# Block-turned attention heads: the diagonal blocks copied by GpSimd, and one store for a tile's attention output

## The chip, the cores and the metric

The kernel runs on one core of a Trainium2 chip. The metric is device time in microseconds (us) of one execution; lower is better. The kernel before was timed three times: 2246.76, 2250.20 and 2251.48 us, median 2250.2 us.

## The reference

Two layers of a hybrid encoder are applied to a prompt of 1024 positions and a sample of 256 positions, all in float32. Each layer normalises its input, projects it once (`h @ w_in`), and runs four groups side by side: attention, a Fourier mix, spatial gating and a cross-attention into memory tokens. Each group is multiplied by a gate, the four are joined, projected by `w_out`, normalised and added to the input. The change touches the attention group alone:

```python
def self_attention(q, k, v):          # 8 query heads, 2 key/value heads, width 64
    ...
    def one_block(qblk):              # 128 queries at a time
        s = jnp.einsum('bqkgd,bskd->bkgqs', qblk, k, preferred_element_type=jnp.float32) * scale
        p = jax.nn.softmax(s, axis=-1)
        return jnp.einsum('bkgqs,bskd->bqkgd', p.astype(v.dtype), v)
    ...
o_att = self_attention(q, k, v) * jax.nn.silu(ag)
```

## The kernel before

The 1280 positions are ten tiles of 128: tiles 0 to 7 are the prompt, 8 and 9 the sample. Per layer the kernel does the spatial gating, the Fourier groups and the memory heads, then the projections for attention (`attention_qkv`, `attention_gates`), then the attention tiles (`attention`), and then the output product (`output`), which begins beside tiles 8 and 9. Results of the groups go to DRAM arrays `o_d[0..15]`, of 128 rows (channels) by 1280 positions each; `o_d[0..3]` are attention's. `output` reads them back (`load_o`, L910), attention's last.

In `attention` a prompt tile takes eight steps, one per head, in the order 2, 0, 3, 1, 6, 4, 7, 5 (L850). Heads 0 to 3 share key/value head `kv` 0, heads 4 to 7 `kv` 1; `j` is the head's number in its four. A step multiplies queries and keys on TensorE (`score`, L761), takes the row maximum on VectorE (L764) and the exponential on ScalarE (L766). Then the 128 by 1024 probabilities must be turned so that keys lie on the partitions (`turn`). Heads with `j` 0 or 1 are turned by TensorE (L791) and copied out by ScalarE (L796). Heads with `j` 2 or 3 are block-turned: VectorE's transpose (L776) turns only within 32 by 32 blocks and writes a tile `blocks`, and after the second of the two heads sixteen DMAs (L782) move `blocks` into `pd`, each 32 partitions by 2 KB (64 KB). Group `a` of 32 partitions and block `b` go to group `b` of `pd`; in the four moves of `r` = 0, `a` equals `b` and the partitions stay the same. So a prompt tile has 32 such DMAs, and a layer 256.

The product with the values (`values`, L833) of a tile runs during the steps of the tile after it, in four parts at steps 0, 2, 4 and 6 (L878 to 884). Parts 0 and 1 read `pt` (heads turned on TensorE), parts 2 and 3 read `pd`. The last part is followed by `finish`: VectorE multiplies the sum by the gate (L838), and four DMAs (L840) store the four 128 by 128 pieces into `o_d[0..3]`, 64 KB each.

All DMAs are issued by SyncE (SP) from one queue in order, so an issue that waits holds all behind it. That queue holds also the load of the next queries (L721, step 3) and of the gate (L800, step 4). GpSimd does two things per tile here: the low part of the queries (L727, step 1) and the spreading of the reciprocal row sums (L807, step 7).

`blocks` has two buffers (tag `a8`), `pt` and `pd` four together (`a16`). TensorE's order in this stage is the program's (L1056); the other engines' orders, SP's too, come out of a planner that simulates the program when it is built, so an operation that is moved can change the order of its neighbours.

Of the kernel before, what the change touches and what calls it, by code (L numbers as in the profile page):

```python
# [15 lines left out]
P = 128  # L16
# [3 lines left out]
SEQ = 1024  # L20
DEC = 256
# [53 lines left out]
def trunk_kernel(  # L75
# [10 lines left out]
    nc = tc.nc  # L86
# [11 lines left out]
    def a8(shape, dt=F32R):  # L98
        return sb.tile(shape, dt, tag="a8", bufs=2, name=uid("a8_"))

    def c4(shape, dt=F32):
        return sb.tile(shape, dt, tag="c4", bufs=N_C4, name=uid("c4_"))

    def c2(shape, dt=F32):
        return sb.tile(shape, dt, tag="c2", bufs=N_C2, name=uid("c2_"))
# [7 lines left out]
    def st(shape, tag="st", bufs=16):  # L113
        return sb.tile(shape, F32, tag=tag, bufs=bufs, name=uid("st_"))

    def mm(shape, dt=F32):
        return ps.tile(shape, dt, tag="mm", bufs=4, name=uid("mm_"))
# [18 lines left out]
    def dram(name, shape):  # L136
        return tc.dram_tile(shape, F32, name=name)

    def bcast(src, n):
        return src.unsqueeze(0).to_broadcast([P, n])  # L140
# [139 lines left out]
    def memory_prep(l, delay):  # L280
        gb = c4([P, D])
        nc.sync.dma_start(gb, bcast(mem_g[l], D))
        mT = [[c4([P, 2, 512], F32R) for _ in range(4)] for _ in range(2)]
        done = set()

        def put(mt, xs):
            pt = transpose_rows(xs)
            s = slice(mt * P, (mt + 1) * P)
            for k in range(4):
                split(mT[0][k][:, :, s], mT[1][k][:, :, s], pt[:, 2 * k:2 * k + 2, :])  # L290
            done.add(mt)
            S.tick(8 * TT)

        for mt in range(4):
            src = mem_prompt if mt < 2 else mem_sample
            x_sb = c4([P, D])
            nc.sync.dma_start(x_sb, src[(mt % 2) * P:(mt % 2 + 1) * P, :])
            xs = norm_rows(x_sb, gb)
            S.later(delay * (mt + 1), lambda mt=mt, xs=xs: put(mt, xs))
        return mT, done  # L300
# [81 lines left out]
    def fourier_setup(l):  # L382
        cs = c2([P, 2, P])
        nc.sync.dma_start(cs, c_dft)
        wf = c2([P, 4, P])
        nc.sync.dma_start(wf, w_fourier[l])
        pos = []
        for i in range(2):
            raw = wr([P, 2, 2, 256])
            nc.sync.dma_start(raw, c_pos[:, 2 * i:2 * i + 2])  # L390
            m = [c4([P, 2, 2, 256], F32R) for _ in range(2)]
            split(m[0], m[1], raw)
            pos += [[x[:, k] for x in m] for k in range(2)]
        cw = [c4([P, 4, 2, P], F32R) for _ in range(2)]
        for q in range(2):
            acc = s2([P, 4, P])
            nc.tensor.matmul(acc.rearrange("p g d -> p (g d)"), cs[:, q, :],
                             wf.rearrange("p g d -> p (g d)"), start=True, stop=True)
            split(cw[0][:, :, q, :], cw[1][:, :, q, :], acc)
        return cw, pos  # L400
# [139 lines left out]
    def memory_setup(l):  # L540
        out = []
        for src in (mk_d[l], mv_d[l]):
            hl = []
            for c in range(2):
                raw = wr([P, 2, 512])
                nc.sync.dma_start(raw, src[:, 2 * c:2 * c + 2])
                t = [c4([P, 2, 512], F32R) for _ in range(2)]
                split(t[0], t[1], raw)
                hl.append(t)
            out.append(hl)  # L550
        return out

    def memory_head(l, hT, h, o_d, mk, mv):
        w = slab("in", l, SLAB_MEM[h])
        for g in range(3):
            memory_unit(w, hT, h, g, o_d, mk, mv)
# [152 lines left out]
                S.tick(ROWS_COST)  # L709
        return q_d, kT, v8, v2  # L710

    def attention(l, q_d, kT, v8, v2, ag, o_d):

# [53 lines left out]
        def turn(t, h):  # L769
            e = tiles[t]  # L770
            kv, j = h // 4, h % 4
            p = e.pop(h)
            if e["prompt"] and j >= 2:
                if j == 2:
                    e["blocks"] = a8([P, 4, 8, 2, 32], F32)
                nc.vector.transpose(e["blocks"][:, :, :, j - 2].rearrange("p b k q -> p k b q"),  # L776
                                    p.rearrange("p (k b q) -> p k b q", b=4, q=32))
                if j == 3:
                    for r in range(4):
                        for a in range(4):  # L780
                            b = (a + r) % 4
                            nc.sync.dma_start(  # L782
                                e["pd"][32 * b:32 * b + 32, a, kv].rearrange("p k j q -> p (k j q)"),
                                e["blocks"][32 * a:32 * a + 32, b].rearrange("p k j q -> p (k j q)"))
                return
            for half in range(2 if e["prompt"] else 1):
                kn = 4 if e["prompt"] else 2
                pt = mm([P, 4, P])
                for kk in range(kn):
                    c0 = (half * 4 + kk) * P  # L790
                    nc.tensor.transpose(pt[:, kk, :], p[:, c0:c0 + P], ident)  # L791
                if e["prompt"]:
                    dst = e["pt"][:, half * 4:half * 4 + kn, kv, j, :]
                else:
                    dst = e["pt"][kv][:, :, j, :]
                nc.scalar.copy(dst, pt[:, :kn])  # L796
# [38 lines left out]
        def finish(t):  # L835
            e = tiles.pop(t)
            o = c2([P, 4, P])
            nc.vector.tensor_tensor(o, e["acc"], e["gt"], ALU.mult)  # L838
            for j in range(4):
                nc.sync.dma_start(o_d[j][:, t * P:(t + 1) * P], o[:, j, :])  # L840

        load_q(0)
        load_q(1)
# [11 lines left out]
        for n, (t, i, h) in enumerate(work):  # L855
# [14 lines left out]
            if i in (3, 5) and t + 1 < NT:  # L870
                turn_q(qhl, tiles[t + 1]["qT"], (i - 3) // 2)
            turn(t, h)
            if i == 7:
                for fs in todo:
# [142 lines left out]
        S.later(3.5 * (t - 1) - 9, lambda t=t: start_tile(t))  # L1017
    S.tick(0)
    for l in range(DEPTH):
        o_d = [dram(f"o{l}_{c}", [P, SEQ + DEC]) for c in range(16)]  # L1020
        cst = c4([P, 2, 4, P])
        nc.sync.dma_start(cst[:, 0], w_spatial[l])
        nc.sync.dma_start(cst[:, 1].rearrange("p h q -> p (h q)"), bcast(b_spatial[l], 512))
        vg = st([P, 4], tag="vg", bufs=1)
        nc.sync.dma_start(vg, v_g[l])
        sgu_pair(l, hT, 0, o_d, cst[:, 0], cst[:, 1], vg)
        four = []
        early = lambda: four.extend(fourier_setup(l))
        prep = []
        if l == 0:  # L1030
            sgu_pair(l, hT, 1, o_d, cst[:, 0], cst[:, 1], vg, lambda: prep.extend(memory_prep(0, 6)))
            m1 = memory_prep(1, 9)
            memory_kv(0, *prep, lambda: None)
            memory_kv(1, *m1, early)
        else:
            sgu_pair(l, hT, 1, o_d, cst[:, 0], cst[:, 1], vg, early)
        cw, pos = four
        for h in range(4):
            fourier_group(l, hT, h, o_d, cw, pos)
        mk, mv = memory_setup(l)  # L1040
        for h in range(4):
            memory_head(l, hT, h, o_d, mk, mv)
        q_d, kT, v8, v2 = attention_qkv(l, hT)
        ag = [dram(f"ag{l}_{t}", [P, 4, P]) for t in range(NT)]
        att = attention(l, q_d, kT, v8, v2, ag, o_d)
        gates = attention_gates(l, hT, ag)
        for i in range(7):
            next(gates)
            if i == 4:
                S.drain()  # L1050
        next(att)
        next(gates)
        last = l == DEPTH - 1
        out_hT = []
        out = output(l, o_d, xin if l == 0 else xmid, xout if last else xmid, out_hT)
        with tc.manual_schedule(engines={mybir.EngineType.PE}):  # L1056
            next(att)
            next(gates, None)
            for t, h in att:
                if t == 0 and h % 2 == 0:  # L1060
                    next(gates, None)
                if t >= 8:
                    next(out)
        for _ in out:
            pass
        hT = out_hT[0] if out_hT else None
# [89 lines left out]
```

## Time and profile before

| | us |
|---|---|
| median of three runs | 2250.2 |
| the profiled execution, its own time | 2251.54 |
| its span in the trace | 2249.5 |
| TensorE busy (matmul) | 2161.9 (96%) |
| VectorE busy | 1124.4 (50%) |
| ScalarE busy | 852.9 (38%) |
| GpSimd busy | 243.6 (11%) |
| mean granted TensorE clock | 0.987 |

Times in the trace count from the start of the span. An instruction is named by engine, line and the tiles that it writes and reads. A number in square brackets behind an instruction is the time for which its engine stood idle before it, with what ended the wait. "PE" is TensorE, "PEld" its weight loads, "DVE" VectorE, "ACT" ScalarE, "POOL" GpSimd, "SPq" the queue of SyncE. The prompt's attention tiles lie at about 715 to 938 us in layer 0 and 1776 to 2003 us in layer 1.

### The profile page before, as it was taken

Reading aid. Unit: us, or ns where it says so; the run is one execution under the profiler, and the core shown is the slowest. Engines: PE = TensorE matmul, PEld = TensorE weight load, DVE = VectorE, ACT = ScalarE, POOL = GpSimd, SP = SyncE. Lnnn points to the kernel's source line nnn. Section 1 sums busy time; section 2 is a strip of 40 time slices with the busy share of each in tenths; the row PEclk is TensorE's granted clock in tenths of the full one; section 3 lists DMA queues with packets and bytes.
Section 4 is the critical chain, followed back from the end, with each engine's and each line's share of the span. In section 5 each row is a group of like instructions: output and inputs, shape, how many; then the busy total and the mean of one; then the engine's idle time right before and its main releaser. Section 6 shows DMA issues by size and latency. Waiting matters only on the chain.

```text
span 2249.5 us, 33414 instructions
## 1 busy us (share of the span) xinstructions
PE 2161.9 (96%) x12872; PEld 1842.0 (82%) x12872; DVE 1124.4 (50%) x1972; ACT 852.9 (38%) x1935; POOL 243.6 (11%) x416
## 2 busy tenths in 40 slices
PE   7999999999999988999999999999999988999997
PEld 7898988888998656678888988888899866667885
DVE  6344344445573666534464343445467365643445
ACT  6133332334322656542264222234342365654121
POOL 2010000000141000000062000000014000000005
PEclk9999999999999999999999999999999998999999
DMA  4123321201122544532342121021112344453234
GB/s 172 59 97 131 131 92 57 99 31 55 59 78 69 129 115 122 146 103 85 103 163 86 57 80 57 31 99 42 51 55 79 91 111 110 123 146 99 91 106 140
DMA packets 120782, 210.95 MB, mean 94 GB/s; under 512 B 20400, under 2 KB 55600, under 8 KB 120624
## 3 DMA queue, kind: packets, MB, share of 16 engines
q1 hardware_dynamic: 120624, 208.82, 29.9%
q8 instruction: 102, 1.67, 0.3%
q14 instruction: 56, 0.46, 0.1%
HBM read 129.05 MB, written 46.14 MB: 78 GB/s over the span
## 4 chain that ended last, share of the span: by engine, by line
PE 76%; SPq 9%; DMA 5%; DVE 4%; issue 2%; ACT 2%; POOL 2%; DVEq 0%; POOLq 0%; ACTq 0%
PE mm L248 34%; PE mm L926 13%; PE mm L261 12%; SPq L782 7%; PE mm L833 3%; PE s L761 3%; PE mm L311 2%; PE mm L327 1%; PE s L422 1%; PE s L408 1%; PE s L576 1%; DMA wr<-o 1%; PE mm L609 1%; DMA a<-a 1%; SPq L840 1%
## 5 line engine op out<-in xcount | busy, mean ns | idle before, releaser
L248 PE MATMUL mm<-a,ws 128*128 128x512 f32 (+1 forms) x4032 | 795.1, 355 | 0.0
L248 PEld LDWEIGHTS mm<-a,ws 128*128 128x128 f32 x4032 | 663.6, 189 | 102.5 <-issue 0.5
L926 PE MATMUL mm<-ws,a 128*128 128x512 f32 x1632 | 380.6, 392 | 2.6 <-ACT c L933 2.6
L926 PEld LDWEIGHTS mm<-ws,a 128*128 128x128 f32 x1632 | 303.9, 188 | 67.4 <-ACT c L933 3.6
L261 PE MATMUL mm<-ws,a 128*128 128x256 f32 x2400 | 302.0, 286 | 0.0
L261 PEld LDWEIGHTS mm<-ws,a 128*128 128x128 f32 x2400 | 294.8, 194 | 0.5 <-DVE a L234 0.2
L764 DVE TENSOR_REDUCE st<-s 128x1 f32<-128x1024 f32 (+1 forms) x160 | 170.0, 1063 | 148.8 <-PE s L761 148.7
L833 PE MATMUL mm<-a,c 128*64 128x256 f32 x1024 | 148.0, 413 | 41.3 <-DMA a<-a 41.2
L273 ACT ACTIVATE c<-mm 128x512 f32<-128x512 f32 (+1 forms) x96 | 50.7, 528 | 322.8 <-PE mm L248 319.0
L766 ACT ACTIVATE c<-s,st 128x1024 f32<-128x1024 f32 (+1 forms) x160 | 159.0, 994 | 35.7 <-DVE st L764 34.9
L761 PE MATMUL s<-c,c 128*128 128x512 f32 (+1 forms) x576 | 167.8, 410 | 2.5 <-ACT c L766 1.9
L274 DVE SCALAR_TENSOR_TENSOR c<-c,mm 128x512 f32<-128x512 f32 (+1 forms) x96 | 57.2, 595 | 217.8 <-ACT c L273 217.8
L833 PEld LDWEIGHTS mm<-a,c 128*64 128x64 f32 x1024 | 77.7, 145 | 100.8 <-issue 59.1
L166 ACT ACTIVATE ws<-wr,pre_g 128x256 fp32r<-128x256 f32 x304 | 126.6, 505 | 22.2 <-DMA wr<-in_w_in_dram 16.0
L761 PEld LDWEIGHTS s<-c,c 128*128 128x128 f32 x576 | 101.7, 194 | 37.7 <-issue 18.4
L167 DVE SCALAR_TENSOR_TENSOR ws<-wr,pre_g,ws 128x256 fp32r<-128x256 f32 x304 | 128.6, 483 | 2.6 <-ACT ws L166 2.5
L935 DVE TENSOR_TENSOR c<-c,mm 128x512 f32<-128x512 f32 x120 | 80.9, 682 | 83.9 <-PE mm L926 83.9
L148 POOL TENSOR_SCALAR st<-st 128x1 f32<-128x1 f32 (+3 forms) x120 | 26.7, 223 | 743.5 <-DVE st L654 453.4
L150 POOL TENSOR_TENSOR st<-st,mhalf 128x1 f32<-128x1 f32 (+3 forms) x120 | 99.8, 832 | 9.9
L776 DVE STREAM_TRANSPOSE a<-c 128x1024 f32<-128x1024 f32 x64 | 79.2, 1237 | 31.9 <-DMA a<-a 27.7
L144 DVE TENSOR_TENSOR ws<-wr,ws 128x1024 fp32r<-128x1024 f32 x48 | 57.0, 1221 | 67.0 <-ACT ws L143 66.9
L143 ACT CAST ws<-wr 128x1024 fp32r<-128x1024 f32 x48 | 48.1, 1049 | 101.6 <-PE mm L926 84.4
(120 smaller groups left out, 2213.7 us busy)
## 6 DMA issues: line engine op xcount, KB each, us to landing
wr<-in_w_in_dram SPq DMA_DIRECT2D x76, 512.0 KB, 4.3
a<-a SPq DMA_DIRECT2D x512, 64.0 KB, 2.0
wr<-in_w_out_dram SPq DMA_DIRECT2D x32, 512.0 KB, 4.4
wr<-o SPq DMA_DIRECT2D x64, 256.0 KB, 3.0
c<-in_x_prompt_dram SPq DMA_DIRECT2D x16, 512.0 KB, 6.2
o<-c SPq DMA_DIRECT2D x32, 256.0 KB, 2.0
wr<-in_w_mem_kv_dram SPq DMA_DIRECT2D x16, 512.0 KB, 4.1
q<-c SPq DMA_DIRECT2D x40, 128.0 KB, 1.7
```

Source lines behind the costliest of these rows:

```text
L150: nc.gpsimd.tensor_tensor(r, m, mhalf[:, :n], ALU.pow)
L166: nc.scalar.activation(w[:, 0, kk], raw[:, k], AF.Copy, scale=g)
L167: nc.vector.scalar_tensor_tensor(w[:, 1, kk], raw[:, k], g, fv(w)[:, 0, kk], ALU.mult, ALU.subtract)
L248: nc.tensor.matmul(acc[:, :n], w[:, a, k, c * P:(c + 1) * P], hT.t[g][b][:, k, :], start=i == 0, stop=i == 3 * KC - 1)
L261: nc.tensor.matmul(acc[:, :256], hT.t[g][a][:, k, tt * P:(tt + 1) * P], w[:, b, k, :], start=i == 0, stop=i == 3 * KC - 1)
L761: nc.tensor.matmul(s[:, c0:c0 + n], e["qT"][:, h, :], kT[kg][b][:, kv, :], start=b == 0, stop=b == 1)
L764: nc.vector.tensor_reduce(nm, s[:, :nk], axis=AX.X, op=ALU.max, negate=True)
L766: nc.scalar.activation(p[:, :nk], s[:, :nk], AF.Exp, bias=nm, accum_out=e["rs"][:, j, kv:kv + 1])
L782: nc.sync.dma_start(e["pd"][32 * b:32 * b + 32, a, kv].rearrange("p k j q -> p (k j q)"), e["blocks"][32 * a:32 * a + 32, b].rearrange("p ...
L833: nc.tensor.matmul(out, vt, src, start=kt == 0, stop=kt == last)
L926: nc.tensor.matmul(acc, oT[g][c][:, a, tt * P:(tt + 1) * P], w[:, b, c, :], start=j == 0, stop=j == 11)
L935: nc.vector.tensor_tensor(ys, ys, acc, ALU.add)
```

## The change

The four DMAs with `r` = 0 become four GpSimd copies, in the same loop and for the same data; the twelve others stay DMAs of SP. The array of attention's output becomes one DRAM array of 128 by 4 by 1280, and `finish` stores a tile by one DMA of 256 KB (128 partitions, four runs of 512 B each) in place of four. `output` reads the same pieces as before, from slices of that array.

```diff
-    def attention(l, q_d, kT, v8, v2, ag, o_d):
+    def attention(l, q_d, kT, v8, v2, ag, o_att):
...
                     for r in range(4):
                         for a in range(4):
                             b = (a + r) % 4
-                            nc.sync.dma_start(
-                                e["pd"][32 * b:32 * b + 32, a, kv].rearrange("p k j q -> p (k j q)"),
-                                e["blocks"][32 * a:32 * a + 32, b].rearrange("p k j q -> p (k j q)"))
+                            dst = e["pd"][32 * b:32 * b + 32, a, kv].rearrange("p k j q -> p (k j q)")
+                            src = e["blocks"][32 * a:32 * a + 32, b].rearrange("p k j q -> p (k j q)")
+                            if r == 0:
+                                nc.gpsimd.tensor_copy(dst, src)
+                            else:
+                                nc.sync.dma_start(dst, src)
...
-            for j in range(4):
-                nc.sync.dma_start(o_d[j][:, t * P:(t + 1) * P], o[:, j, :])
+            nc.sync.dma_start(o_att[:, :, t * P:(t + 1) * P], o)
...
-        o_d = [dram(f"o{l}_{c}", [P, SEQ + DEC]) for c in range(16)]
+        o_att = dram(f"o{l}_att", [P, 4, SEQ + DEC])
+        o_d = [o_att[:, c, :] for c in range(4)] + [dram(f"o{l}_{c}", [P, SEQ + DEC]) for c in range(4, 16)]
```

## Rows read from the trace of the kernel before

**Rows 1.** The page: busy time, and the chain that ended last by line.

```profile
PE 2161.9 (96%) x12872; PEld 1842.0 (82%) x12872; DVE 1124.4 (50%) x1972; ACT 852.9 (38%) x1935; POOL 243.6 (11%) x416
...
PE mm L248 34%; PE mm L926 13%; PE mm L261 12%; SPq L782 7%; PE mm L833 3%; PE s L761 3%; PE mm L311 2%; PE mm L327 1%; PE s L422 1%; PE s L408 1%; PE s L576 1%; DMA wr<-o 1%; PE mm L609 1%; DMA a<-a 1%; SPq L840 1%
```

**Rows 2.** The waits: engine, line, waited for, us in total, times, longest.

```profile
PE mm L833 <- DMA a<-a: 41.2, 14, 4.4
...
DVE a L776 <- DMA a<-a: 27.7, 13, 3.8
```

**Rows 3.** Busy time by stretch: from wait to wait, six tiles a layer, then two single ones.

```profile
core 0: us, PE busy (x) PEld busy (x) DVE busy (x) ACT busy (x) POOL busy (x), PEclk, DMA share, GB/s
...
764.41:914.63 150.22, 129.98 (x840) 89.49 (x841) 96.59 (x92) 93.06 (x168) 11.37 (x12) 0.97 0.47 116
1826.24:1979.37 153.13, 135.38 (x840) 92.75 (x841) 95.78 (x91) 90.07 (x165) 11.36 (x12) 0.92 0.46 114
...
764.41:789.12 24.71, 20.88 (x140) 14.48 (x141) 16.00 (x16) 15.76 (x29) 1.90 (x2) 1.00 0.49 118
...
1878.55:1905.69 27.14, 23.69 (x141) 16.06 (x141) 15.99 (x16) 15.01 (x27) 1.89 (x2) 0.88 0.44 108
```

**Rows 4.** Busy time by stretch, as rows 3, after the last wait of each layer.

```profile
914.63:938.20 23.57, 23.26 (x138) 16.44 (x139) 10.81 (x16) 10.70 (x26) 1.91 (x2) 0.93 0.49 121
1979.37:2003.00 23.63, 23.32 (x138) 16.56 (x139) 11.80 (x17) 12.84 (x30) 1.90 (x2) 0.93 0.47 116
```

**Rows 5.** Timeline of SP's queue over one tile of layer 0: start, us, instruction.

```profile
837.51 10.04 SPq L782 DMA_DIRECT2D a<-a  x15
847.66 0.53 SPq L721 DMA_DIRECT2D c<-q  x1
848.23 0.46 SPq L800 DMA_DIRECT2D c<-ag  x1
848.78 0.51 SPq L782 DMA_DIRECT2D a<-a  x1
849.39 1.98 SPq L840 DMA_DIRECT2D o<-c  x4
851.42 12.10 SPq L782 DMA_DIRECT2D a<-a  x18
```

**Rows 6.** All issues of L782: duration in ns (min/median/max), and time to landing.

```profile
L782 SPq DMA_DIRECT2D a<-a x512: 507/589/1923, 735.3 to 2002.5; - x171
...
DMA to landing us min/median/max: 1.9/2.0/4.7
```

**Rows 7.** Timeline of VectorE in the same tile: last of `kv` 1, `finish`, next `kv` 0.

```profile
844.94 1.24 DVE L776 STREAM_TRANSPOSE a<-c 128x1024 f32<-128x1024 f32 x1
...
847.94 0.68 DVE L838 TENSOR_TENSOR c<-mm,c 128x512 f32<-128x512 f32 x1
...
854.53 1.23 DVE L776 STREAM_TRANSPOSE a<-c 128x1024 f32<-128x1024 f32 x1
```

**Rows 8.** Timeline of TensorE at the wait of that tile, and at one in tiles 8, 9.

```profile
858.81 0.65 PE L833 MATMUL mm<-a,c 128*64 128x256 f32 x2
863.11 2.84 PE L833 MATMUL mm<-a,c 128*64 128x256 f32 x14 [3.65 <-DMA a<-a]
...
2015.94 3.01 PE L926 MATMUL mm<-ws,a 128*128 128x512 f32 x12 [1.60 <-ACT c L933]
```

**Rows 9.** Timeline of GpSimd and VectorE where they work at the same time, attention.

```profile
822.16 0.61 POOL L807 COPY c<-st 128x512 f32<-128x512 f32 x1 [17.06 <-DVE st L805]
822.27 1.22 DVE L764 TENSOR_REDUCE st<-s 128x1 f32<-128x1024 f32 x1 [0.17 <-PE s L761]
...
827.06 1.23 DVE L764 TENSOR_REDUCE st<-s 128x1 f32<-128x1024 f32 x1 [0.34 <-PE s L761]
827.33 1.28 POOL L727 TENSOR_TENSOR c<-c,c 128x512 fp32r<-128x512 f32 x1 [4.57 <-ACT c L726]
```

**Rows 10.** The same at the end of layer 0, and the durations of L959.

```profile
1152.15 1.29 POOL L951 TENSOR_TENSOR c<-c,c 128x512 f32<-128x512 f32 x1
1152.22 2.43 DVE L959 SCALAR_TENSOR_TENSOR c<-c,st,c 128x512 f32<-128x512 f32 x2 [1.22 <-POOL st L150]
...
L959 DVE SCALAR_TENSOR_TENSOR c<-c,st,c x40: 737/751/1783, 1130.9 to 2245.5; 128x512 f32<-128x512 f32 x40
```

More of the change, by code (lines that the diff above doesn't have):

```diff
@@ L1044, in trunk_kernel @@
         ag = [dram(f"ag{l}_{t}", [P, 4, P]) for t in range(NT)]
-        att = attention(l, q_d, kT, v8, v2, ag, o_d)
+        att = attention(l, q_d, kT, v8, v2, ag, o_att)
         gates = attention_gates(l, hT, ag)
```

## The prediction

> **What bounds the kernel now.** I read the page first. TensorE is busy for 96% of the span, so as a whole this is a TensorE kernel; but in the chain that ended last, one line of SP's queue, L782, has 7% of the span [rows 1]. 7% of 2249.5 us is 157 us in which the end of the program hung on SP issuing the block moves. That is a share of the chain and not a gain: if the issues go faster, TensorE's own work takes their place. So the second view is the waits: TensorE stood still for the block moves 14 times, 41.2 us in all, always at L833; VectorE waited 27.7 us for the same moves before its block transposes (L776), since `blocks` has two buffers [rows 2].
>
> The third view is the stretches from one wait's end to the next. Twelve of them, six a layer, hold a tile each. They last 303.35 us (150.22 + 153.13) of which TensorE is busy 265.36 (129.98 + 135.38); the difference, 38.0 us, is twelve of the fourteen waits, and 3.2 us are the first of each layer [rows 3]. The same 140 matmuls take 20.88 us at a granted clock of 1.00, which is 2.4 GHz, and up to 23.69 us where it was 0.88, so that a part of the stretch went at 1.2 GHz [rows 3]. TensorE did nothing else in those stretches than in the others; what came before the lower clock is the wait. VectorE has 16.0 us of work per tile and ScalarE 15.0 to 15.8, less than TensorE's 20.88, so neither would hold a tile of 20.9 us.
>
> The fourth view is SP's queue in one tile [rows 5]. It is full: 15 block moves from 837.51 to 847.55, the two loads, one move, the four stores, and 18 moves from 851.42. That is 0.67 us for a move (10.04 / 15, and 12.10 / 18), 1.98 us for the stores, 0.53 and 0.46 for the loads. 32 x 0.67 + 1.98 + 0.99 = 24.4 us per tile, and the stretch at full clock lasts 24.7 us [rows 3]. So **in the prompt's attention SP's issuing is the bound, and TensorE, which needs 20.9 us, waits for the rest.**
>
> **The change, part by part.**
>
> *Four of sixteen moves leave SP.* Per tile 24 moves stay: 24 x 0.67 = 16.1 us, with the loads and the store (below) 17.5 to 19.1 us. That is under 20.9, so SP has a reserve and TensorE becomes the bound. But a reserve on average isn't enough, the moves of `kv` 1 must land in time. I follow one tile through three views [rows 5, 7, 8]. Its `kv` 1 blocks are ready at 846.18 (L776 at 844.94 for 1.24). TensorE asks for them at 859.46, the end of the two matmuls at 858.81, so it can give them 13.3 us. Before, SP was still at work on `kv` 0 at 846.18, sent one move at 848.78 and the others from 851.42; TensorE went on at 863.11. After, the `kv` 0 moves (12 x 0.67 = 8.0 us) and the loads (1.0 us) fit in the 11.3 us between the `kv` 0 blocks (one period of 20.88 before 854.53 + 1.23, so 834.88) and 846.18; SP is free then. If the planner keeps its order, one move goes first, then the store, which must wait for L838 (till 847.94 + 0.68 = 848.62), and eleven moves are queued behind that wait. The store's issue takes 0.46 to 1.98 us (below), so the eleven begin at 849.1 to 850.6, the last 10 x 0.67 later, at 855.8 to 857.3, and it lands 2.0 us after its issue [rows 6]: 857.8 to 859.3. TensorE asks at 859.46. **The waits of 41.2 us go, with 0.2 to 1.7 us to spare.** What is late next is nothing that I can see for those 20.9 us: the stretch at full clock has no other wait. VectorE's wait of 27.7 us goes too; it counts for nothing of its own, since TensorE waited at the same time.
>
> *TensorE's clock.* The twelve stretches at full clock would be 12 x 20.88 = 250.56 us of TensorE's work in place of 265.36, so 14.8 us go as well if the clock stays at 1.00 [rows 3]. After the last wait of each layer comes another stretch at 0.93, 23.3 us busy [rows 4]; 7% of that is 1.6 us each, 3.2 us. Bounds: none of these 18.0 us comes back, or all. I take all, because the stretch from 764.41, behind one of the two first waits (1.6 us in the mean), ran at 1.00 [rows 3], and I expect no longer ones.
>
> *The copies on GpSimd.* A copy writes 512 elements per partition. The nearest row is L807, a copy of 512 per partition, 0.61 us; the upper end is L727 with two inputs, 1.28 us [rows 9]; the lower end is nothing, since only 32 partitions are busy. Four take 2.4 us (0 to 5.1) and are done 849 to 851, ahead of the twelve DMAs, which hide them. That cover is 13.3 us wide; it would be used up only at 3.3 us a copy. Per tile GpSimd gets 4.9 us on top of 1.9 [rows 3]. Behind the copies in its queue stand L807, which may come 2.4 us later (TensorE reads its result at step 2 of the next tile, two steps on), and L727, not needed for two steps either. Cost 0.
>
> *Four stores become one.* No store or load of the trace has four runs per partition. Lower end: the cost of L800, a load of 256 KB with one run per partition, 0.46 us [rows 5]; upper end: the four stores as before, 1.98 us. What SP saves here is at most 1.5 us per tile, and hidden once SP isn't the bound. I take the middle; both ends are in the walk above. When it lands doesn't matter: L910 reads it after the products of the three other groups.
>
> *What stays.* At tiles 8 and 9 TensorE waits for loads of the output product that stand behind the last moves in SP's queue (one of 1.60 us [rows 8]). SP gets there earlier by 2.7 us (4 x 0.67) and TensorE too. I keep back 3.0 us for waits that come up there.
>
> *A rule against it.* Where GpSimd and VectorE worked at once with L764, L764 took 1.22 and 1.23 us, as alone [rows 9]. Where VectorE had two inputs in SBUF, at the layer's end, two L959 beside L951 took 2.43 us in place of 2 x 0.75 [rows 10]. In attention no VectorE operation has two SBUF inputs. The Trainium skill, page "SBUF — State Buffer", section "SBUF: two separate sides", says that VectorE and GpSimd share a pair of ports by an exclusive lock, and that the loser blocks fully. By the rows the copies cost VectorE nothing, by that rule taken without its condition they would cost what the third rival has; the L959 rows agree with the rule.
>
> *Sum.* 41.2 + 14.8 + 3.2 - 3.0 = 56.2 us. The profiled execution had 2251.54 us, its span lacks 2.0 of it: 2251.5 - 56.2 = 2195.3. The median of the runs lies 1.3 us below the profiled one: **2194 us**.
>
> **The rivals.**
>
> 1. *A wait remains.* The planner puts the store ahead of all twelve moves and its issue is dear: 850.6 + 11 x 0.67 + 2.0 = 860.0, 0.5 us late; with one long issue (up to 1.92 us for 0.59 [rows 6]) 1.8. For it: the margin was 0.2 us at the dear end. Against: at the cheap end it is 1.7. Some 1.3 us at 14 places give 18 us back, with the clock at 1.00 as after the first waits: 2212 us; with half of the clock's loss 2221.
> 2. *Nothing changes.* The moves' landing and not their issue sets the time, so fewer issues help nothing: 2250 us. Against: landing takes 2.0 us while the issues stand back to back for 24.4, and the DMA engines are busy 0.47 [rows 3]. The skill's page "DMA: Bandwidth & Descriptors", section "Issuing engines are not separate DMA queues", calls the saving in issue time usually small beside the DMA itself; these rows speak against that here.
> 3. *Slower: the copies hold VectorE.* If they lock L764 and L776 out, 8 copies x 0.61 = 4.9 us per tile fall into VectorE's order, which sets off each exponential. It decides once more than 59.2 / 16 = 3.7 us of these count. All of it: 16 x 4.9 = 78 us, 2272 us. Against: rows 9. For: no row shows L776 beside GpSimd.
>
> **How the numbers follow.** Forecast 0.70, first rival 0.18, second 0.03, third 0.06; 0.03 for a planner's order that costs some us, still faster. The range holds the forecast with its ends: 2194 less the 3.0 kept back, less 3.2 if waits like the 1.60 us go in both layers, less 3.4 for the fastest run before (2246.8 against 2250.2), gives 2184; the first rival at its dear end, 2221, and 3 more give 2224. A measurement here tells 0.2% (4.5 us) from no change. Faster: 0.70 + 0.18 + 0.03 = 0.91, same 0.03, slower 0.06.
>
> **What would show it.** Right: no wait of L833 for block moves over 1.3 us, tiles of 20.9 to 21.5 us, granted clock 0.98 or more in both prompt stretches, gaps in SP's queue. The part on order is wrong if the waits stay at L833 with the store just ahead of the moves; the part on copies if L764 or L776 grow beyond 1.25 us, or L833 waits for GpSimd. A tile still at 24 us would make the whole reading wrong.

## The result and the profile after

The changed kernel takes 2190.87 us in the median of four runs (2188.82 to 2192.31), against 2250.84 us before. The ratio is 0.9741, with a 95% interval of 0.9724 to 0.9757. The profiled execution had 2190.76 us, 60.8 us less than the one before; the prediction's sum was 56.2. The predicted time was 2194 us.

TensorE's busy share rose to 98%. SP's line of the block moves, 7% of the chain that ended last in [rows 1], is no longer among the parts that the page lists; the chain is TensorE's. The page of the changed kernel, busy time and the chain by line:

```profile
PE 2140.2 (98%) x12872; PEld 1832.7 (84%) x12872; DVE 1122.5 (51%) x1972; ACT 853.1 (39%) x1935; POOL 324.7 (15%) x544
...
PE mm L248 35%; PE mm L928 16%; PE mm L261 12%; PE s L761 6%; PE mm L836 5%; PE mm L794 3%; PE mm L311 2%; PE mm L327 1%; PE s L422 1%; PE s L408 1%; PE s L576 1%; PE mm L609 1%; POOL c L953 1%; PE s L217 1%; DVE c L961 1%
```

The values product is line 836 now, the block moves that are left are line 787, the copies 785, the store 842, `finish`'s multiplication 841. In the groups of instructions of the changed kernel (busy time, mean ns | idle time before them, and what ended it) the values product waits 5.2 us in all, for ScalarE, where it waited 41.2 us for DMAs [rows 2]. VectorE's block transpose, which waited 27.7 us for DMAs, waits for none:

```profile
L836 PE MATMUL mm<-a,c 128*64 128x256 f32 x1024 | 127.9, 389 | 5.2 <-ACT a L799 5.2
...
L776 DVE STREAM_TRANSPOSE a<-c 128x1024 f32<-128x1024 f32 x64 | 79.0, 1235 | 2.5 <-ACT c L766 2.5
```

The stretches that answer to [rows 3 and 4], in the changed kernel: one tile, the passage from tile 7 to tile 8 in layer 0, six tiles of layer 1 less 0.8 us, and the passage in layer 1 (length, TensorE busy, ..., granted clock, DMA share, GB/s):

```profile
781.77:802.05 20.28, 20.28 (x142) 14.29 (x141) 15.72 (x16) 15.01 (x27) 6.76 (x11) 1.00 0.46 116
...
882.40:908.00 25.60, 22.27 (x131) 15.57 (x130) 16.08 (x24) 17.67 (x40) 8.15 (x10) 0.93 0.59 162
1794.60:1915.50 120.90, 120.90 (x839) 85.17 (x838) 93.77 (x90) 89.68 (x161) 40.28 (x60) 1.00 0.46 116
1915.50:1940.00 24.50, 20.74 (x125) 14.44 (x124) 15.55 (x23) 16.19 (x35) 7.13 (x9) 0.93 0.60 164
```

A tile takes 20.28 us, all of it TensorE's work, at 2.4 GHz throughout. At the passage to tile 8 TensorE is idle for 3.3 and 3.8 us of the stretch, and part of it runs at 1.2 GHz.

SP's queue over one tile of the changed kernel, beside [rows 5], then VectorE and GpSimd at the end of the `kv` 1 blocks, and TensorE's product that reads them:

```profile
781.33 11.13 SPq L787 DMA_DIRECT2D a<-a  x13
792.55 0.57 SPq L842 DMA_DIRECT2D o_att<-c  x1
793.18 6.97 SPq L787 DMA_DIRECT2D a<-a  x11
800.25 0.52 SPq L721 DMA_DIRECT2D c<-q  x1
800.87 0.40 SPq L803 DMA_DIRECT2D c<-ag  x1
...
790.68 1.23 DVE L776 STREAM_TRANSPOSE a<-c 128x1024 f32<-128x1024 f32 x1
791.84 0.65 DVE L841 TENSOR_TENSOR c<-mm,c 128x512 f32<-128x512 f32 x1
...
791.98 2.56 POOL L785 COPY a<-a 32x512 f32<-32x512 f32 x4 [8.04 <-DVE a L776]
794.60 0.61 POOL L810 COPY c<-st 128x512 f32<-128x512 f32 x1
797.45 1.28 POOL L727 TENSOR_TENSOR c<-c,c 128x512 fp32r<-128x512 f32 x1 [2.24 <-ACT c L726]
...
804.58 1.73 PE L836 MATMUL mm<-a,c 128*64 128x256 f32 x14
```

The blocks are ready at 791.91. One move is issued, the store follows at 792.55, and eleven moves take 6.97 us (0.634 each): the last starts at 799.5 and lands at about 801.5, with the 2.0 us of [rows 6]. TensorE's own chain reaches the product that needs it at about 804.9, the second pair of matmuls after 804.58. SP rests ahead of each set of blocks (13 moves at 0.634 are 8.2 of the 11.13 us in the first row); its issues come to 24 x 0.634 + 0.57 + 0.92 = 16.7 us of a tile's 20.28. The four copies are done at 794.5.

### The profile page after: what moved, and what is told of

Its sections match the earlier page's. It is cut to its first block, busy times and chain, and to the rows that moved or that the text cites. A ratio compares the mean times of both kernels' runs of the same rounds, so it can differ in the third digit from the quotient of the medians.

```text
span 2189.0 us, 33399 instructions
## 1 busy us (share of the span) xinstructions
PE 2140.2 (98%) x12872; PEld 1832.7 (84%) x12872; DVE 1122.5 (51%) x1972; ACT 853.1 (39%) x1935; POOL 324.7 (15%) x544
## 4 chain that ended last, share of the span: by engine, by line
PE 87%; DMA 3%; DVE 3%; ACT 3%; POOL 2%; issue 2%; SPq 1%; DVEq 0%; POOLq 0%; ACTq 0%
PE mm L248 35%; PE mm L928 16%; PE mm L261 12%; PE s L761 6%; PE mm L836 5%; PE mm L794 3%; PE mm L311 2%; PE mm L327 1%; PE s L422 1%; PE s L408 1%; PE s L576 1%; PE mm L609 1%; POOL c L953 1%; PE s L217 1%; DVE c L961 1%
## 5 line engine op out<-in xcount | busy, mean ns | idle before, releaser
L261 PE MATMUL mm<-ws,a 128*128 128x256 f32 x2400 | 304.2, 287 | 0.0
L261 PEld LDWEIGHTS mm<-ws,a 128*128 128x128 f32 x2400 | 296.8, 195 | 0.5 <-DVE a L234 0.2
L764 DVE TENSOR_REDUCE st<-s 128x1 f32<-128x1024 f32 (+1 forms) x160 | 170.0, 1062 | 123.2 <-PE s L761 123.2
L836 PE MATMUL mm<-a,c 128*64 128x256 f32 x1024 | 127.9, 389 | 5.2 <-ACT a L799 5.2
L836 PEld LDWEIGHTS mm<-a,c 128*64 128x64 f32 x1024 | 68.8, 137 | 55.7 <-issue 19.7
L785 POOL COPY a<-a 32x512 f32<-32x512 f32 x128 | 80.2, 627 | 199.1 <-DVE a L776 141.7
L953 POOL TENSOR_TENSOR c<-c,c 128x512 f32<-128x512 f32 x40 | 55.8, 1395 | 272.8 <-ACT c L948 272.7
```

Source lines behind the costliest of these rows:

```text
L261: nc.tensor.matmul(acc[:, :256], hT.t[g][a][:, k, tt * P:(tt + 1) * P], w[:, b, k, :], start=i == 0, stop=i == 3 * KC - 1)
L764: nc.vector.tensor_reduce(nm, s[:, :nk], axis=AX.X, op=ALU.max, negate=True)
L785: nc.gpsimd.tensor_copy(dst, src)
L836: nc.tensor.matmul(out, vt, src, start=kt == 0, stop=kt == last)
```

## The experiments

Each was timed beside the kernel before. The table gives the ratio with its 95% interval, and what the values product, and that line alone, waited for in the profile.

| run | us | ratio | values product waits, us |
|---|---|---|---|
| changed kernel | 2190.87 | 0.9741 [0.9724, 0.9757] | 5.2, ScalarE |
| copies alone | 2192.55 | 0.9739 [0.9716, 0.9761] | 1.9, ScalarE |
| store alone | 2235.93 | 0.9933 [0.9908, 0.9957] | 30.8, block moves |
| two copies of four | 2198.85 | 0.9774 [0.9751, 0.9797] | 2.8, block moves |
| four moves issued by GpSimd | 2190.50 | 0.9729 [0.9713, 0.9746] | 4.9, ScalarE |
| tiny DMAs added | 2201.28 | 0.9778 [0.9764, 0.9793] | 12.5, DMAs |
| copies three times | 2280.02 | 1.0131 [1.0111, 1.0150] | 55.4, GpSimd |
| dear copies | 2191.78 | 0.9739 [0.9724, 0.9753] | 2.6, ScalarE |
| later product | 2190.31 | 0.9732 [0.9717, 0.9746] | 5.1, ScalarE |
| splits on GpSimd | 2185.51 | 0.9712 [0.9696, 0.9727] | none |
| changed kernel again | 2187.39 | 0.9717 [0.9701, 0.9733] | the same two waits, 2.2 and 2.4 |

**Copies alone.** The copies stay, the store is four DMAs again.

```diff
-            nc.sync.dma_start(o_att[:, :, t * P:(t + 1) * P], o)
+            for j in range(4):
+                nc.sync.dma_start(o_att[:, j, t * P:(t + 1) * P], o[:, j, :])
```

> Theory (SP's issuing was the bound, TensorE is now): SP has 24 x 0.67 + 1.98 + 0.99 = 19.1 us of issuing per prompt tile, still under the 20.3 us that TensorE takes in the changed kernel, so this is as fast as the whole change: 2189 to 2196 us, and no wait of L833 for block moves over 1 us. Rival (the single store gives much of the gain, since the moves of kv 1 stand behind it): 2205 to 2225 us, with waits left at the values product in each tile.

Measured: 2192.55 us, no wait for block moves. Its interval covers the changed kernel's; on top of the copies the store gains nothing that this measurement can tell. (TensorE's wait for ScalarE is only in another place here: 6.9 us in all at the output product, L929, where the changed kernel has 0.6.)

**Store alone.** All sixteen moves are DMAs of SP, the store is one.

```diff
-                            if r == 0:
+                            if r < 0:
```

> Theory (SP's issuing is the bound): per prompt tile 32 x 0.67 + 0.57 + 0.99 = 23.0 us of issuing against 24.4 before, so SP stays the bound and each of 16 tiles gains 1.4 us, 22 us in all: 2220 to 2235 us, with waits at the values product of about 2 us a tile. Rival (the store matters not at all, being off the path): 2247 to 2253 us.

Measured: 2235.93 us, 15 us less than the kernel before beside it (2251.47); the expectation's edge was 2235, and its 22 us of gain were too many. SP's queue of this kernel is still full, 31 moves without a gap, and TensorE still waits once a tile:

```profile
823.43 0.58 SPq L842 DMA_DIRECT2D o_att<-c  x1
824.06 20.43 SPq L787 DMA_DIRECT2D a<-a  x31
844.59 0.53 SPq L721 DMA_DIRECT2D c<-q  x1
845.16 0.46 SPq L803 DMA_DIRECT2D c<-ag  x1
...
812.68 1.91 PE L836 MATMUL mm<-a,c 128*64 128x256 f32 x14 [2.98 <-DMA a<-a]
835.06 1.91 PE L836 MATMUL mm<-a,c 128*64 128x256 f32 x14 [1.53 <-DMA a<-a]
```

So the two parts of the change don't add: the store is worth 15 us where SP is the bound, and nothing that can be told where the copies have freed it.

**Two copies of four.** 28 moves per tile stay with SP.

```diff
-                            if r == 0:
+                            if r == 0 and a < 2:
```

> Only the copies of a = 0 and 1 are made by GpSimd, 28 moves stay with SP. Theory (SP's issuing against TensorE's work): 28 x 0.67 + 0.57 + 0.99 = 20.3 us, just TensorE's 20.3, so nearly the whole gain: 2190 to 2205 us. Rival (each move taken away saves the same amount by its transfer and landing): half of the way from the store-only kernel to the changed one, 2205 to 2215 us.

Measured: 2198.85 us. Against the store alone, the first two copies per set bring 37 us and the next two 8. That is a bound that changes hands, not a saving per move. With 28 moves it has not changed hands in full: four tiles take 84.73 us, 21.2 each, against 20.28 in the changed kernel.

```profile
762.85:847.58 84.73, 83.14 (x561) 58.39 (x561) 63.41 (x60) 59.81 (x109) 17.26 (x24) 1.00 0.50 125
```

**The four moves issued by GpSimd.** Same transfers as with the store alone, another issuer.

```diff
-                                nc.gpsimd.tensor_copy(dst, src)
+                                nc.gpsimd.dma_start(dst, src)
```

> The four moves of r = 0 are DMAs again, with the same bytes, but issued by GpSimd. Theory (what bound the kernel before was SP's time to issue): SP has the same 24 moves per tile as in the changed kernel, so its gain stays, if GpSimd's own issue takes under 2 us (the trace has no such DMA): 2190 to 2205 us. Rival (what bound it was the transfers, their landing or the DMA engines): the transfers are those of the store-only kernel, and the time is the store-only kernel's, 2230 to 2240 us.

Measured: 2190.50 us, the changed kernel's time. The moves and their bytes are those of the store alone, their landing is no sooner, and the 45 us are gone: what was bound was SP's issuing. All such issues of this kernel (ns, min/median/max) and their landing, which is 1.0 us later than for SP's moves and hidden here:

```profile
L785 POOL DMA_DIRECT2D a<-a x128: 498/498/781, 736.8 to 1931.1; - x128
...
DMA to landing us min/median/max: 1.9/3.0/5.4
```

**Tiny DMAs.** The opposite: SP issues eight more DMAs per tile that move next to nothing.

```diff
+        scr = dram(f"scr{l}", [P, 64 * 16])
...
                             if r == 0:
                                 nc.gpsimd.tensor_copy(dst, src)
+                                n = 8 * t + 4 * kv + a
+                                nc.sync.dma_start(scr[32 * a:32 * a + 32, 16 * n:16 * n + 16],
+                                                  e["blocks"][32 * a:32 * a + 32, a, 0, 0, 0:16])
```

> The changed kernel, and SP issues four more DMAs per set, of 64 bytes a partition in 32 partitions, into an array that nobody reads. Theory (SP's time to issue, paid per DMA): if a tiny issue costs as much as a move, SP has 32 x 0.63 to 0.67 + 1.6 = 21.8 to 23.0 us per tile and the time goes back to 2215 to 2240 us, with waits at the values product; if a tiny one costs the 0.32 us of the shortest issue before, SP has 19.3 us and nothing changes. Rival (bytes): the bytes are 1/32 of the moves that were removed, so the time stays at 2188 to 2195 us though SP's queue is full.

Measured: 2201.28 us, between the two values that were written down for this theory, and outside the rival's. Waits at the values product are back, 12.5 us. The profile puts 8.0 of them down to the tiny DMAs, but the product reads nothing that these write: at 805.21 it had the last of the moves in front of them, issued at about 803.0 and landed 2.0 us later. What the tiny DMAs take is SP's time, and so the moves come late. An issue of 2 KB in all takes 0.42 us in the median, against 0.59 for 64 KB:

```profile
L788 SPq DMA_DIRECT2D scr<-a x128: 318/419/1269, 719.8 to 1944.4; - x128
...
799.80 3.75 SPq L791 DMA_DIRECT2D a<-a  x6
803.65 1.93 SPq L788 DMA_DIRECT2D scr<-a  x4
...
805.21 1.91 PE L840 MATMUL mm<-a,c 128*64 128x256 f32 x14 [1.21 <-DMA scr<-a]
```

With 0.48 us each (1.93 us for four, the row at 803.65) SP has 24 x 0.63 + 8 x 0.48 + 1.5 = 20.5 us per tile, just over TensorE's 20.3. With 1/32 of the bytes an issue keeps 0.48 of 0.63 us: most of its cost does not go with the bytes.

**Copies three times.** This was to show how wide the cover of the copies is.

```diff
-                                nc.gpsimd.tensor_copy(dst, src)
+                                for _ in range(3):
+                                    nc.gpsimd.tensor_copy(dst, src)
```

> Each copy is made three times. Theory (the copies are hidden by 13.3 us and cost VectorE nothing): a set takes 7.7 us in place of 2.55, GpSimd has 17 us per tile, under 20.3: 2189 to 2197 us, L764 still at 1.22 us. Rival (GpSimd's copies lock VectorE out): 10 us more per tile fall on VectorE, up to 16 x 10 = 160 us, 2230 us or more, and L764 or the block transposes L776 are longer than 1.25 us.

Measured: 2280.02 us, slower than before. The theory's number is missed, and the rival's mechanism isn't there either: L764 keeps its time, in the changed kernel 170.0 us for 160 of them and here 169.8, and so does L776, 1.24 us at 806.85 beside two copies (groups of instructions of this kernel; line 837 is the values product, 786 the copies):

```profile
L764 DVE TENSOR_REDUCE st<-s 128x1 f32<-128x1024 f32 (+1 forms) x160 | 169.8, 1061 | 164.0 <-PE s L761 164.0
...
L837 PE MATMUL mm<-a,c 128*64 128x256 f32 x1024 | 148.1, 414 | 56.7 <-POOL a L786 55.4 <-ACT a L800 1.3
```

TensorE waits for GpSimd, though GpSimd's work per tile, 24 x 0.61 + 1.9 = 16.5 us, is less than 20.3. GpSimd's timeline over one tile of this kernel tells why (then VectorE and TensorE in the same tile):

```profile
803.35 2.56 POOL L786 COPY a<-a 32x512 f32<-32x512 f32 x4 [6.39 <-DVE a L776]
805.97 0.61 POOL L811 COPY c<-st 128x512 f32<-128x512 f32 x1
806.53 1.27 POOL L786 COPY a<-a 32x512 f32<-32x512 f32 x2
808.87 1.28 POOL L727 TENSOR_TENSOR c<-c,c 128x512 fp32r<-128x512 f32 x1 [1.08 <-issue]
810.22 1.27 POOL L786 COPY a<-a 32x512 f32<-32x512 f32 x2
813.02 10.57 POOL L786 COPY a<-a 32x512 f32<-32x512 f32 x16 [1.53 <-PE mm L817]
...
806.85 1.24 DVE L776 STREAM_TRANSPOSE a<-c 128x1024 f32<-128x1024 f32 x1
811.67 1.23 DVE L776 STREAM_TRANSPOSE a<-c 128x1024 f32<-128x1024 f32 x1
...
815.95 0.65 PE L837 MATMUL mm<-a,c 128*64 128x256 f32 x2
818.33 1.94 PE L837 MATMUL mm<-a,c 128*64 128x256 f32 x14 [1.74 <-POOL a L786]
```

Eight of the twelve `kv` 1 copies run, with L811 and L727 between. Then GpSimd stands idle for 1.53 us with four of them undone, so in its program these must stand behind copies of the next tile's `kv` 0 blocks, which wait for L776 (811.67, done at 812.90; L817, which the row names, ended 0.06 us later). So the last come among the sixteen after 813.02, and TensorE, which asked at about 816.6, went on at 818.33. GpSimd had the time for them; what held TensorE was their place in the queue. Why the planner interleaves the repeats was not tested; that they write the same place one after another is a guess.

**Dear copies.** The same question without repeats: one instruction per block with two inputs, 1.03 us in the median.

```diff
+    zero = sb.tile([P, 1], F32, name="zero")
+    nc.vector.memset(zero, 0.0)
...
-                                nc.gpsimd.tensor_copy(dst, src)
+                                nc.gpsimd.tensor_tensor(dst, src, zero[32 * a:32 * a + 32].to_broadcast([32, 512]), ALU.add)
```

> Each copy is an addition of zero with two inputs, one instruction per block as in the changed kernel, so that the copies cost about 1.28 us each (as L727) in place of 0.61. Theory (the copies are hidden, and the three-fold copies were slow because their repeats stood in GpSimd's queue behind L727 and the next blocks): a set takes 5.1 us, still under 13.3: 2188 to 2196 us. Rival (GpSimd's work itself reaches the path, or holds VectorE): 2.6 us a set more, some 40 to 80 us in all, 2230 us or more.

Measured: 2191.78 us, no change, with 3.4 us more of GpSimd's time per tile (8 x (1.03 - 0.61)). The copies are hidden, as the theory has it, up to 4.1 us a set; the expectation had 5.1, and the three-fold copies' 7.7 us a set, in one piece, was not tried.

**Later product.** The new waits, at the passage to tile 8, come from ScalarE. In the changed kernel, ScalarE and then TensorE:

```profile
895.51 2.80 ACT L915 ACTIVATE a<-wr 128x256 fp32r<-128x256 f32 x6 [1.03 <-DMA wr<-o]
898.22 0.56 ACT L799 COPY a<-mm 128x512 f32<-128x512 f32 x1
...
898.84 3.26 PE L836 MATMUL mm<-a,c 128*64 128x256 f32 x14 [2.40 <-ACT a L799]
```

Six splits for the output product (L915) stand ahead of the copy that TensorE needs, and the first of them waits 1.03 us for a load.

```diff
-                if t >= 8:
+                if t > 8 or (t == 8 and h >= 2):
```

> The changed kernel, with the first output product begun two steps of tile 8 later. Theory (the wait of 2.4 to 2.8 us at the passage from tile 7 to tile 8, for ScalarE's copy L799, comes from the loads and splits of the output product which the planner puts ahead of it): the waits of L836 for L799 go in both layers, 2180 to 2189 us. Rival (the planner puts the splits there whatever the program's order, or the wait only moves to the first products): 2188 to 2196 us, and waits of 2 us or more stay between tile 7 and the end of tile 9.

Measured: 2190.31 us; the waits of L836 for L799 stay, 2.53 and 2.58 us:

```profile
900.05 1.94 PE L836 MATMUL mm<-a,c 128*64 128x256 f32 x14 [2.53 <-ACT a L799]
1934.63 1.94 PE L836 MATMUL mm<-a,c 128*64 128x256 f32 x14 [2.58 <-ACT a L799]
```

The rival holds for this shift: the planner puts the splits there although the program asks for them two steps later. Behind both waits the fourteen matmuls take 1.94 us, the time at full clock; in the changed kernel they took 3.26 behind 2.40 us.

**Splits on GpSimd.** The high parts of the first product's inputs go to GpSimd (24 instructions, 1.28 us in the mean).

```diff
-                        nc.scalar.activation(o[:, 0], raw[:, cc], AF.Copy, scale=0.5)
+                        if qt == 2:
+                            nc.gpsimd.tensor_scalar(o[:, 0], raw[:, cc], 0.5, None, ALU.mult)
+                        else:
+                            nc.scalar.activation(o[:, 0], raw[:, cc], AF.Copy, scale=0.5)
```

> The changed kernel, with the high parts of the first product's inputs made by GpSimd in place of ScalarE (20 instructions in all). Theory (TensorE waits 2.4 and 2.8 us at the passage to tile 8 for ScalarE's copy L799, which stands in ScalarE's queue behind six such parts, and behind the load that they wait for): these two waits go, and some 2 us of lowered clock each: 2180 to 2187 us. Rival (the parts are in the way on GpSimd too, ahead of the block copies of tile 7 or the row sums): TensorE waits for GpSimd at the values product of tile 7, 2188 us or more.

> The changed kernel itself, beside the variant on the same chip: 2188 to 2193 us.

Measured: 2185.51 us against 2187.39 us for the changed kernel on the same chip (0.6 below what was expected of it). The intervals overlap, so that it is faster is not shown. The two waits for L799 are gone, as the theory said; in layer 0 another came up in their place, at the first products of the output stage (line 931 here), and with it a lower clock:

```profile
920.54 4.61 PE L931 MATMUL mm<-ws,a 128*128 128x512 f32 x12 [4.16 <-ACT c L938]
```

## Why the prediction was right

*The bound.* SP's issuing was the bound and TensorE became it. The GpSimd-issued moves and the tiny DMAs show this from both sides, and two copies of four show the point where it changes: 28 moves with the store and the loads are 20.3 us, TensorE's own, and tiles of 21.2. The second rival, that landing sets the time, falls with them. The Trainium skill's page "DMA: Bandwidth & Descriptors", in "Issuing engines are not separate DMA queues", calls the saving of issue time usually small beside the DMA itself; here an issue is 0.59 us beside 2.0 to the landing, and since the issues stood back to back, issuing from a second engine was worth 45 us.

*The sum, term by term.* Six tiles of layer 0 took 150.22 us, of layer 1 153.13 [rows 3]; six tiles of 20.28 us are 121.7. That is 60.0 us less in both. Of it 38.0 are the waits and 14.8 the clock, as the sum had them. The other 7.2 us the sum lacked: it took TensorE's 20.88 us of work per tile as fixed, and it fell to 20.28. Before, the product that was broken by the wait showed 0.65 us for its two matmuls and 1.91 for the fourteen others, 2.56 together; unbroken, sixteen show 1.95. The difference is 0.61 us per wait: in a row the matmuls overlap (one alone lasts 0.379 us in the profile, sixteen in a row 1.95), and those before and after a wait don't. The kernel before, then the changed one:

```profile
810.93 0.65 PE L833 MATMUL mm<-a,c 128*64 128x256 f32 x2
814.06 1.91 PE L833 MATMUL mm<-a,c 128*64 128x256 f32 x14 [2.48 <-DMA a<-a]
...
799.05 1.95 PE L836 MATMUL mm<-a,c 128*64 128x256 f32 x16
```

The stretches' lengths bear the total out; how it is shared between wait and work goes by ends of matmuls that the profile models. With the first waits of each layer (3.2 us, and 0.61 each) the prompt's part is 64.4 us. So the prediction's sign of tiles of 20.9 to 21.5 us was not met; they are shorter.

*The end of the stage.* The sum counted 3.2 us for a full clock after the last waits [rows 4] and kept back 3.0 for waits at tiles 8 and 9. New waits did come, 2.40 and 2.82 us, but by another mechanism: the prediction expected TensorE to wait for loads behind SP's moves, and it waits for ScalarE, whose queue holds splits that wait for a load. The clock at the passage is still 0.93 in the changed kernel, so the 3.2 us are not seen. A wait alone does not settle the clock: behind waits of 2.53 and 2.58 us the later product ran at full clock, and the changed kernel run again did so in layer 0 and not in layer 1 (the kernel before has both as well: 1.91 us for the fourteen behind a wait of 3.65 at 838.60, 3.35 behind 1.87 at 1826.24):

```profile
899.30 1.94 PE L836 MATMUL mm<-a,c 128*64 128x256 f32 x14 [2.17 <-ACT a L799]
...
1931.02 2.99 PE L836 MATMUL mm<-a,c 128*64 128x256 f32 x14 [2.43 <-ACT a L799]
```

64.4 - 60.8 = 3.6 us are missing, and little of that lies here. From the third matmul of the last product that waited before (914.63 us; about 886.4 in the changed kernel) to the first product behind the output product (L261, at 1172.32 and 1145.30) the two kernels take 257.7 and 258.9 us in layer 0; in layer 1, to the end of the span (from 1979.37 and about 1919.5), 270.1 and 269.5. Another 1.3 us lie ahead of layer 0's attention tiles, whose first transposes (L733) start at 714.93 us in place of 713.67; executions of one kernel differ by as much. So the sum lacked 8.4 us (7.2 and twice 0.61) and had 3.8 too many (0.2 gained for this part, 3.6 lost). The two errors are of opposite sign and leave 4.6, from 56.2 to 60.8: the mechanism of the forecast is borne out, and that it came within 4 us of the median is partly luck.

*The walk through one tile.* It gave 0.2 to 1.7 us to spare; measured are about 3.4 (804.9 - 801.5). Three entries were too high: the price of a move, 0.634 us where the queue has rests, for 0.67; the store's issue (0.575 us in the median, near the lower end of 0.46 to 1.98; the walk's range took both); and the wait for `finish`, which the planner now puts right behind the block transpose: 791.84 to 792.49 in place of 2.4 us after it. That order couldn't be read from the trace before. The order of the first rival, the store ahead of all twelve moves, did not come.

*The copies.* Priced at 0.61 us, measured 0.607 in the median. Hidden, as said, and dear copies show it. That L764 keeps its time (1.22 us) speaks against the third rival. For L776 the changed kernel tells nothing, since no L776 runs beside a copy in it; the three-fold copies do, where L776 takes 1.24 us beside them.

The prediction's "no VectorE operation has two SBUF inputs" holds for attention's own operations. It left out the output product's splits (L916, inputs `wr` and `a`), which begin beside tile 7's copies, and there the two are slower:

```profile
882.72 3.60 POOL L785 COPY a<-a 32x512 f32<-32x512 f32 x4 [2.89 <-PE mm L816]
883.30 0.69 DVE L916 SCALAR_TENSOR_TENSOR a<-wr,a 128x512 fp32r<-128x512 f32 x1 [0.70 <-ACT a L915]
...
895.96 1.68 DVE L916 SCALAR_TENSOR_TENSOR a<-wr,a 128x256 fp32r<-128x256 f32 x2 [0.56 <-ACT a L915]
897.17 0.95 POOL L810 COPY c<-st 128x512 f32<-128x512 f32 x1
```

Four copies take 3.60 us in place of 2.56, L810 0.95 in place of 0.61, and two of the splits 1.68 together, where the shortest alone takes 0.41. That agrees with the lock of the Trainium skill's page "SBUF — State Buffer", section "SBUF: two separate sides", whose conditions include that VectorE's operation has two inputs in SBUF; L764 has one input, in PSUM, and L776 one, and neither grew. TensorE's values product waits for none of this.

"The cover is 13.3 us wide" holds for the copies' time alone. Three-fold copies, at 7.7 us a set, fit into it and still cost 89 us over the changed kernel, since a queue that runs in order has a cover only as wide as the first thing behind which they are put.

*What stays open.* Why the planner places the splits where it does was not pursued further than the two variants. What decides whether the clock falls behind a wait is not shown. Whether an issue's time is SP's own or that of the queue which it fills, the runs don't tell apart; either way it is paid per issue, and a second issuer takes it off.

## What to carry to other kernels

Count the issues of one queue per period and set their time beside the work of the engine that should be the bound; where the queue's sum equals the measured period, taking issues off it pays until the sums meet, and nothing after. Two edits that relieve the same queue need not add up: here either took some of the same gain, and on top of the copies the store brought nothing that could be told. When work moves to an idle engine that runs in order, look at what stands ahead of and behind it in that engine's queue, and not only at whether its time fits.

## What was not expected

A DMA of 2 KB costs SP 0.42 us to issue and one of 64 KB 0.59, while one store with four runs in each of 128 partitions costs 0.575, against 0.43 for each of the four that it replaces (the four took 1.98 us [rows 5]). An issue from GpSimd took 0.50 us. A GpSimd copy of 512 elements takes the same 0.61 us on 32 partitions as on 128 [rows 9]. A wait in the middle of a row of sixteen matmuls cost 0.61 us beyond its idle time. GpSimd's copies took longer beside VectorE operations with two inputs in SBUF (3.60 us in place of 2.56 for four), and the same beside L764 and L776.
